# Feed-forward gates written in block order by ScalarE, output weights in two runs, memory tokens copied in that order and begun sooner

## The chip, the cores and the metric

One of the eight cores of a Trainium2 chip runs the kernel. The metric is the device time of one execution in microseconds; of several runs the median is given. One profiled execution gives the rows that are quoted.

## The reference

Two layers of a decoder trunk work on x, 256 tokens of width 1024, in f32. Each layer has a feed-forward step, a mixer of three branches and a second feed-forward step, each with a norm before and after:

```
x += 0.5 * post1(SwiGLU1(pre1(x)))
h  = pre2(x)
x += post2( W_o( sum_i sigmoid(G_i h) * P_i(branch_i(h)) ) )
x += 0.5 * post3(SwiGLU2(pre3(x)))

def swiglu(h, w_in, w_out):
    a, b = split(h @ w_in, 2)            # 2 x 2816 columns
    return (silu(a) * b) @ w_out         # 2816 rows
```

The third branch is cross-attention into 256 memory tokens mem. Its keys and values are rms_norm(mem, mem_g) @ w_mem_kv, with weights and gain of the layer and the same mem in both layers.

## The kernel before

**Tiles and streams.** The 256 tokens are two tiles of 128 (t = 0 and 1). Each is a stream, a Python generator that goes through both layers; the main loop lets the two take turns, stream 0 a few steps ahead, so that a weight tile that was loaded serves both. A step is, for one token tile, one weight tile's products in TensorE. `now` counts the steps. Smaller jobs (the memory tokens' keys and values, attention, compression) are generators in a background list; one piece of them runs after each step, and a number that a generator yields is the count of steps until its next piece. `later(n, fn)` runs fn n steps on.

**Weights.** All products are in f32r with three passes: weight high by x high, weight low by x high, weight high by x low. A weight tile is loaded by SP into one of 4 raw buffers (128 x 1024); `split_unit` then makes whi by a cast on ScalarE (L319) and wlo by a subtraction on VectorE (L320). A dry run of the program finds at what step each tile is first wanted; loads go out up to 7 steps ahead of that and splits up to 4 (AHEAD), in this order and as buffers come free. The instruction orders of the other engines follow from the program's order and the scheduler; each engine works its own list in order.

**Feed-forward** (`ffn`). The columns of w_in go in five pairs of 512 and one of 256. For each, `gate` takes the two accumulators pa and pb: ScalarE makes th = tanh(pa r/2) (L570), VectorE makes (th + 1) pa (L571) and then multiplies by a per-token scale and by pb (L575) into one half of `wide`. Every second gate hands `wide` to `turn_beside`, which brings its 128-column blocks to the transposed form that the second product needs.

**Turning without TensorE.** `turn` has VectorE transpose 32 x 32 squares (L433, tile `blocks`), then one step later (AWAY) four DMAs from GpSimd's queue move the squares' rows to their partitions (L439, tile `moved`), and some steps later (SPLIT = 11) the result is used: for the gates cast and subtracted into turnhi and turnlo (L456, L457). Read with steps (32, 1), column 32q + j of a block of 128 ends on partition 4j + q. So the rows of w_out must lie on the partitions in the same order. Together with the order in which `moving` reads the columns of w_in, this makes w_out's 128 rows come in runs: `RUNS` holds the length u, and the load (L305) reads "(k v u) n -> k u v n", with u = 16 for both feed-forward steps (eight runs of 16 rows for each weight tile) and 64 for w_mix_out and two of the branches.

**Memory tokens** (`memory`). It begins when stream 0 is at the fifth output weight of the first feed-forward step of a layer (`begin_layer`). In layer 0, for each of two tiles (mt), SP loads m; three steps on come its norm (L467 and a chain on GpSimd) and `turn` with order (1, 4), where VectorE reads m with a step of four elements, so that tokens' columns end in plain order; 11 steps later `gained` multiplies by the gain (mf, L710) and makes mThi and mTlo (L713, L714), and `keep` stores the turned tile to DRAM (mthere, L696). Layer 1 reads it back. One step after the last tile the products with w_mem_kv begin, four steps for the keys and four for the values, two steps between, each step with 12 products beside those of the streams.

In layer 0 the steps from the beginning to the products are 3 + 11 + 3 + 11 + 1 = 29, in layer 1 6 + 6 + 1 = 13.

Of the kernel before, what the change touches and what calls it, by code (L numbers as in the profile page):

```python
# [27 lines left out]
AF = mybir.ActivationFunctionType  # L28
OP = mybir.AluOpType
AX = mybir.AxisListType  # L30

P = 128
# [23 lines left out]
LANES = 4  # L56
NORM_B, NORM_C = 1, 1
AWAY, SPLIT, RETURN = 1, 11, 6
CONV, BS, CMP, ZC, QS_0, QS_1, QM, PC, YM = 4, 4, 6, 2, 2, 6, 2, 3, 1
ATT_A, ATT_B, ATT_C, ATT_D, ATT_T = 1, 3, 2, 6, 8  # L60
EARLY, RAMP, SCALES, STAGED, SETUP = 6, 10, 5, 8, 30
PACE, PACE_1, PACED = 9, 8, ("nsa", "memory")

RUNS = {"ffn1_w_out": 16, "ffn2_w_out": 16, "w_mix_out": 64, "w_branch_conv": 64, "w_branch_mem": 64}
PRE = ("ffn1_norm_pre", "mix_norm_pre", "ffn2_norm_pre", "mem_norm")

INV_FREQ = [float.fromhex(v) for v in (
# [39 lines left out]
def view(ap, off, dims):  # L107
    if isinstance(ap, Nothing):
        return ap
    return bass.AP(tensor=ap.tensor, offset=ap.offset + off, ap=[list(ap.ap[0])] + [list(d) for d in dims])  # L110
# [16 lines left out]
def lanes_in(ap, c, n=P):  # L127
    return view(ap, c, [[P, n // P], [1, 4], [4, 32]])


def lanes_out(ap, c, dims):
    return view(ap, c, [list(d) for d in dims] + [[32, 4], [1, 32]])


def f32(ap):
    return ap.bitcast(F32)
# [19 lines left out]
def program(tc, nc, pools, a, out, plan):  # L156
# [18 lines left out]
    def bank(name):  # L175
        return psa.tile([P, 512], F32, name=name, tag="a")
# [4 lines left out]
    def gtile(name, dt=F32):  # L181
        return gp.tile([P, 1024], dt, name=name, tag="g")

    def ttile(name, dt=F32):
        return tp.tile([P, 520], dt, name=name, tag="tmp")
# [55 lines left out]
    order, found, ready = [], {}, {}  # L241
# [30 lines left out]
    def load(item, engines=None):  # L272
# [10 lines left out]
        for off, step, name, l, k0, nk, c0, n in parts:  # L283
# [16 lines left out]
            else:  # L300
                src = a[name][l, k0 * P:(k0 + nk) * P, c0:c0 + n]
                if name in RUNS:
                    rows = src.rearrange("(k v u) n -> k u v n", k=nk, u=RUNS[name])
                    for k in range(nk):
# [61 lines left out]
    def later(delay, fn):  # L366
        serial[0] += 1
        deferred.append((now[0] + delay, serial[0], fn))
# [15 lines left out]
    def product(hT, name, l, cols):  # L384
        ps = [bank("acc") for _ in cols]
        for k in range(8):
            parts = [(0, -1, name, l, k, 1, cols[0][0], cols[0][1])]
            hi, lo = unit((name, l, cols[0][0], k), parts)
            for i, (x2, w) in enumerate(((0, hi), (1, hi), (0, lo))):
                for j, p in enumerate(ps):  # L390
                    n = cols[j][1]
                    pinned(nc.tensor.matmul(p[:, :n], lhsT=hT[x2][:, k], rhs=moving(w, j * n, n),  # L392
                                            start=(k == 0 and i == 0), stop=(k == 7 and i == 2)))
            yield 0
        return ps
# [30 lines left out]

    def turn(src, n, finish, wait, order=(32, 1)):
        f = n // 4  # L430
        make = gtile if n > 512 else ttile
        blocks = make("blocks")
        nc.vector.transpose(blocks[:, :n], view(src, 0, [[order[0], 4], [P, n // P], [order[1], 32]]))  # L433
        moved = []

        def away():
            moved.append(make("moved"))
            for q in range(4):
                nc.gpsimd.dma_start(moved[0][:, q * f:(q + 1) * f],  # L439
                                    blocks[q * 32:(q + 1) * 32, :n].rearrange("j (p f) -> j p f", p=4))  # L440

        later(AWAY, away)
        later(wait, lambda: finish(turned_view(moved[0], n)))
        return moved

    def turned_view(moved, n):
        return view(moved, 0, [[32, n // P], [n // 4, 4], [1, 32]])
# [4 lines left out]
    def turn_beside(src, n, put, wait=SPLIT):  # L452
        def split(mv):
            hi, lo = gtile("turnhi", F32R), gtile("turnlo", F32R)
            hv, lv = quarters(hi[:, :n], n // P), quarters(lo[:, :n], n // P)
            nc.scalar.copy(hv, mv)  # L456
            nc.vector.tensor_sub(lv, mv, f32(hv))  # L457
            put(hi, lo)

        turn(src, n, split, wait)  # L460
# [102 lines left out]
    def ffn(t, l, which):  # L563
        w_in, w_out = f"ffn{which}_w_in", f"ffn{which}_w_out"
        hT, (_, r_half, r2_half, _) = yield from prenorm(x[t], f"ffn{which}_norm_pre", l, t == 0 and l == 0 and which == 1)
        gT, wide = [None] * 3, [None]

        def gate(j, n, pa, pb):
            th = ttile("th")
            nc.scalar.activation(th[:, :n], pa[:, :n], AF.Tanh, scale=r_half)  # L570
            nc.vector.scalar_tensor_tensor(th[:, :n], th[:, :n], 1.0, pa[:, :n], op0=OP.add, op1=OP.mult)  # L571
            if j % 2 == 0:
                wide[0] = gtile("wide")
            both, c0 = wide[0], j % 2 * 512
            nc.vector.scalar_tensor_tensor(both[:, c0:c0 + n], th[:, :n], r2_half, pb[:, :n], op0=OP.mult, op1=OP.mult)  # L575
            if j % 2 == 1:
                turn_beside(both, c0 + n, lambda hi, lo: gT.__setitem__(j // 2, (hi, lo)))

        for j in range(5):
            pa, pb = yield from product(hT, w_in, l, [(j * 512, 512), (DFF + j * 512, 512)])  # L580
            gate(j, 512, pa, pb)
        ps = yield from halves(hT, w_in, l, [(2560, 256), (DFF + 2560, 256)])
        gate(5, 256, ps[:, 0:256], ps[:, 256:512])
        y = [bank("y0"), bank("y1")]
        def between(k):
            if k == 4 and t == 0 and which == 1:
                begin_layer(l)

        def lhs(k):
            c = (k % 8) * P  # L590
            return [v[:, c:c + P] for v in gT[k // 8]]

        yield from output(y, w_out, l, 22, lhs, between)
        yield from postnorm(y, t, (f"ffn{which}_norm_post", l), 0.5, which == 2 and l == DEPTH - 1)
# [97 lines left out]
    def keep(mt, gained):  # L692
        def finish(mv):
            gained(mv)
            whole = bass.AP(tensor=mv.tensor, offset=mv.offset, ap=[list(mv.ap[0]), [1, 1024]]) if not dry else mv
            nc.gpsimd.dma_start(mthere[mt], whole)  # L696
        return finish
# [6 lines left out]
    def memory(l):  # L704
        S = shared[l]
        H = []
        for mt in range(2):
            def gained(mv, scale=[mscale[mt][:, i:i + 1] for i in range(4)]):
                hf, hi, lo = gtile("mf"), gtile("mThi", F32R), gtile("mTlo", F32R)
                nc.vector.tensor_tensor(quarters(hf, 8), mv,  # L710
                                        view(gT, PRE.index("mem_norm") * 16 + l * 8, [[1, 8], [0, 4], [0, 32]]),
                                        op=OP.mult)
                nc.scalar.copy(hi, hf)  # L713
                nc.vector.tensor_sub(lo, hf, f32(hi))  # L714
                H.append((tokens_last(hi, lo), scale))

            if l == 0:
                m = gtile("m")
                nc.sync.dma_start(m, a["mem"][0, mt * P:(mt + 1) * P, :])
                yield 3  # L720
                norm_scales(m, 0, mscale[mt])
                turn(m, 1024, keep(mt, gained), SPLIT, (1, 4))
                yield SPLIT
            else:
                back(mt, gained)
                yield RETURN
        yield 1
        ps = [bank("acc") for _ in range(2)]

        def products(c0):  # L730
            for u in range(4):
                hi, lo = unit(("w_mem_kv", l, c0, u), [(0, 512, "w_mem_kv", l, 2 * u, 2, c0, 512)])
                for mt in range(2):
                    product2(ps[mt], H[mt][0], hi, lo, 512, 2 * u, u == 0, u == 3)
                yield 1

        yield from products(0)
        ks = gtile("ks")
        for mt in range(2):
            nc.scalar.activation(lanes_out(ks, mt * P, [[256, 4]]), lanes_in(ps[mt], 0, 512), AF.Copy,  # L740
                                 scale=H[mt][1][0])

        def keys(hi, lo):
            S["km"] = [v.rearrange("p (h m) -> p h m", h=4) for v in (hi, lo)]

        turn_beside(ks, 1024, keys, KEYS)
        yield 2
        ps = [bank("acc") for _ in range(2)]
        yield from products(512)
        S["vm"] = []  # L750
        for mt in range(2):
            vm = gtile("vm", F32R)
            evac_split(vm[:, 0:512], vm[:, 512:1024], ps[mt], H[mt][1][1])
            S["vm"].append(vm)
# [675 lines left out]
```

## Time and profile before

| | us |
|---|---|
| median of 3 runs | 1219.95 |
| the runs | 1216.92, 1219.95, 1220.46 |
| profiled execution, its time | 1217.41 |
| profiled execution, its span | 1215.7 |
| TensorE busy | 1188.8 |
| VectorE busy | 906.1 |
| ScalarE busy | 722.9 |
| GpSimd busy | 175.4 |

The span goes from the first instruction to the last; the time takes in what lies around it. A TensorE product is pipelined with the next, so its row's duration is longer than its step, and a busy TensorE can still be slowed: the starts of the rows tell. In a row of the timeline stand the start in us from the beginning of the span, the duration, engine, line, operation, tiles (out<-in), shapes and count, and in brackets how long the engine was idle before and what ended that. In a row of a stretch stand its bounds and length, the busy us of PE (TensorE), PEld (its weight loads), DVE (VectorE), ACT (ScalarE) and POOL (GpSimd), the mean granted clock of TensorE, the busy share of the DMA engines and GB/s. In a row of waits stand who waited, for whom, the total, the number of times and the longest. In a row of DMA issues stand the number, the size and the median us from issue to landing.

### The profile page before, as it was taken

To read this page: it belongs to the slowest core of one execution; us is meant where nothing else is said; L and a number is where in the kernel's file an instruction comes from. 1 tells how busy PE (TensorE), PEld (TensorE's weight loads), DVE (VectorE), ACT (ScalarE), POOL (GpSimd) and SP (SyncE) were. 2 spreads that over 40 slices of the span, in tenths; PEclk is the share of its full clock that TensorE was granted. 3 is DMA by queue.
4 is the path that set the end of the run, shared out by engine and by line. 5 is a ranking of instruction groups with operands and counts; after the bars stand their busy time and mean duration, and the time that the engine had idled before them with its cause. 6 is when DMAs were issued, how large, how long until landed. Compare 5 with 4: busy or idle time off the path is not lost. (4 is left out here: it accounts for less than half of the span.)

```text
span 1215.7 us, 16522 instructions
## 1 busy us (share of the span) xinstructions
PE 1188.8 (98%) x5776; PEld 1033.6 (85%) x5776; DVE 906.1 (75%) x1157; ACT 722.9 (59%) x1141; POOL 175.4 (14%) x341
## 2 busy tenths in 40 slices
PE   8999989999999999999999999999999999999996
PEld 7888868988888888888888888888888888888885
DVE  7867667888998776666577677577899976767753
ACT  7555346887986564554464454568878754645541
POOL 4001321321111010011011011013012100110100
PEclk9999999999999999999999999999999999999999
DMA  7878887777478657779957789857757677577992
GB/s 249 271 232 213 207 238 246 218 232 214 145 239 218 217 163 231 233 206 215 270 174 236 221 218 268 228 153 225 239 157 224 194 237 211 185 235 218 211 215 71
DMA packets 127090, 260.63 MB, mean 214 GB/s; under 512 B 11200, under 2 KB 30304, under 8 KB 127008
## 3 DMA queue, kind: packets, MB, share of 16 engines
q1 hardware_dynamic: 117088, 234.58, 66.1%
q0 software_dynamic: 9600, 24.47, 8.1%
q8 instruction: 45, 0.74, 0.3%
q10 hardware_dynamic: 320, 0.53, 0.1%
q14 instruction: 37, 0.30, 0.1%
HBM read 235.42 MB, written 2.10 MB: 195 GB/s over the span
## 5 line engine op out<-in xcount | busy, mean ns | idle before, releaser
L320 DVE TENSOR_TENSOR wlo<-raw,whi 128x1024 fp32r<-128x1024 f32 (+2 forms) x441 | 529.9, 1212 | 172.5 <-ACT whi L319 170.0
L319 ACT CAST whi<-raw 128x1024 fp32r<-128x1024 f32 (+2 forms) x441 | 452.8, 1038 | 275.4 <-PE acc L392 132.8
L439 POOL DMA_DIRECT2D moved<-blocks x176 | 96.3, 565 | 665.5 <-DVE blocks L433 259.7
L392 PE MATMUL acc<-whi,hThi 128*128 128x512 f32 x640 | 191.2, 380 | 0.7 <-ACT whi L319 0.6
L392 PE MATMUL acc<-wlo,hThi 128*128 128x512 f32 x640 | 191.7, 380 | 0.1
L392 PE MATMUL acc<-whi,hTlo 128*128 128x512 f32 x640 | 191.0, 380 | 0.0
L380 PE MATMUL acc<-whi,hThi 128*128 128x512 f32 (+1 forms) x480 | 182.7, 381 | 0.7 <-ACT yf L908 0.4
L381 PE MATMUL acc<-wlo,hThi 128*128 128x512 f32 (+1 forms) x480 | 179.4, 374 | 0.9 <-DVE wlo L320 0.9
L382 PE MATMUL acc<-whi,hTlo 128*128 128x512 f32 (+1 forms) x480 | 179.4, 374 | 0.1
L392 PEld LDWEIGHTS acc<-whi,hThi 128*128 128x128 f32 x640 | 120.4, 189 | 18.6 <-ACT whi L319 0.9
L392 PEld LDWEIGHTS acc<-whi,hTlo 128*128 128x128 f32 x640 | 120.7, 189 | 18.2 <-DVE hTlo L496 1.3
L392 PEld LDWEIGHTS acc<-wlo,hThi 128*128 128x128 f32 x640 | 120.9, 189 | 17.4 <-DVE wlo L320 0.5
L381 PE MATMUL y<-wlo,turnhi 128*128 128x512 f32 x352 | 133.8, 380 | 1.6 <-DVE wlo L320 1.6
L380 PE MATMUL y<-whi,turnhi 128*128 128x512 f32 x352 | 133.6, 380 | 0.0
L382 PE MATMUL y<-whi,turnlo 128*128 128x512 f32 x352 | 133.6, 379 | 0.0
L380 PEld LDWEIGHTS acc<-whi,hThi 128*128 128x128 f32 x480 | 90.7, 189 | 12.1 <-ACT yf L908 0.8
L382 PEld LDWEIGHTS acc<-whi,hTlo 128*128 128x128 f32 x480 | 90.7, 189 | 12.2 <-DVE hTlo L496 0.3
L381 PEld LDWEIGHTS acc<-wlo,hThi 128*128 128x128 f32 x480 | 90.8, 189 | 11.6 <-DVE wlo L320 1.5
L457 DVE TENSOR_TENSOR turnlo<-moved,turnhi 128x1024 fp32r<-128x1024 f32 (+1 forms) x42 | 49.2, 1171 | 58.0 <-ACT turnhi L456 57.9
L456 ACT CAST turnhi<-moved 128x1024 fp32r<-128x1024 f32 (+1 forms) x42 | 42.2, 1006 | 66.1 <-DMA moved<-blocks 64.9
L381 PEld LDWEIGHTS y<-wlo,turnhi 128*128 128x128 f32 x352 | 66.5, 189 | 11.6 <-DVE wlo L320 2.3
L380 PEld LDWEIGHTS y<-whi,turnhi 128*128 128x128 f32 x352 | 66.5, 189 | 9.7 <-ACT whi L319 0.4
(304 smaller groups left out, 1443.2 us busy)
## 6 DMA issues: line engine op xcount, KB each, us to landing
raw<-in_ffn_w_in_dram SPq DMA_DIRECT2D x159, 512.0 KB, 4.8
raw<-in_w_mix_in_dram SPq DMA_DIRECT2D x96, 512.0 KB, 4.6
raw<-in_ffn_w_out_dram SPq DMA_DIRECT2D x88, 512.0 KB, 7.0
moved<-blocks POOLq DMA_DIRECT2D x144, 128.0 KB, 4.4
raw<-in_ffn_w_in_dram SPq DMA_DIRECT2D x33, 256.0 KB, 4.0
raw<-in_w_mem_kv_dram SPq DMA_DIRECT2D x16, 512.0 KB, 5.9
raw<-in_w_mix_out_dram SPq DMA_DIRECT2D x16, 512.0 KB, 4.1
raw<-in_cmp_k_w_dram SPq DMA_DIRECT2D x8, 512.0 KB, 4.5
```

The lines of the kernel that those rows point to most:

```text
L319: pinned(nc.scalar.copy(hi[:, c0:c1], raw[:, c0:c1]))
L320: pinned(nc.vector.tensor_sub(lo[:, c0:c1], raw[:, c0:c1], f32(hi[:, c0:c1])))
L380: nc.tensor.matmul(ps, lhsT=xh, rhs=wh, start=start, stop=False, skip_group_check=skip)
L381: nc.tensor.matmul(ps, lhsT=xh, rhs=wl, start=False, stop=False, skip_group_check=skip)
L382: nc.tensor.matmul(ps, lhsT=xl, rhs=wh, start=False, stop=stop, skip_group_check=skip)
L392: pinned(nc.tensor.matmul(p[:, :n], lhsT=hT[x2][:, k], rhs=moving(w, j * n, n), start=(k == 0 and i == 0), stop=(k == 7 and i == 2)))
L439: nc.gpsimd.dma_start(moved[0][:, q * f:(q + 1) * f], blocks[q * 32:(q + 1) * 32, :n].rearrange("j (p f) -> j p f", p=4))
L456: nc.scalar.copy(hv, mv)
L457: nc.vector.tensor_sub(lv, mv, f32(hv))
```

## The change

Three edits go together.

1. In `gate`, ScalarE writes th in the order of the block moves: it reads pa with a step of four (`lanes_in`) and writes four runs of 32 per block (`lanes_out`). A second ScalarE instruction makes half = pa times the per-token scale in the same order. VectorE then makes (th + 1) half from the two tiles, and multiplies by pb, read with a step of four. The turned columns thereby lie in the order of `moving` alone, and w_out's rows come in two runs of 64 instead of eight of 16.
2. A memory tile is copied by ScalarE into mp in that order, and VectorE transposes mp with the ordinary order; `turn` loses its parameter.
3. In layer 0 the second memory tile is begun 5 steps after the first one's turn instead of 11, and in both layers the products begin 3 steps after the last tile instead of 1: 3 + 5 + 3 + 11 + 3 = 25 steps instead of 29 in layer 0, 6 + 6 + 3 = 15 instead of 13 in layer 1.

```diff
+MSTEP, MWAIT = (5, 11), 3
...
-RUNS = {"ffn1_w_out": 16, "ffn2_w_out": 16, "w_mix_out": 64, "w_branch_conv": 64, "w_branch_mem": 64}
+RUNS = {"ffn1_w_out": 64, "ffn2_w_out": 64, "w_mix_out": 64, "w_branch_conv": 64, "w_branch_mem": 64}
...
-    def turn(src, n, finish, wait, order=(32, 1)):
+    def turn(src, n, finish, wait):
...
-        nc.vector.transpose(blocks[:, :n], view(src, 0, [[order[0], 4], [P, n // P], [order[1], 32]]))
+        nc.vector.transpose(blocks[:, :n], view(src, 0, [[32, 4], [P, n // P], [1, 32]]))
...
         def gate(j, n, pa, pb):
             th = ttile("th")
-            nc.scalar.activation(th[:, :n], pa[:, :n], AF.Tanh, scale=r_half)
-            nc.vector.scalar_tensor_tensor(th[:, :n], th[:, :n], 1.0, pa[:, :n], op0=OP.add, op1=OP.mult)
+            nc.scalar.activation(lanes_out(th, 0, [[P, n // P]]), lanes_in(pa, 0, n), AF.Tanh, scale=r_half)
+            half = ttile("half")
+            nc.scalar.activation(lanes_out(half, 0, [[P, n // P]]), lanes_in(pa, 0, n), AF.Copy, scale=r2_half)
+            nc.vector.scalar_tensor_tensor(th[:, :n], th[:, :n], 1.0, half[:, :n], op0=OP.add, op1=OP.mult)
             if j % 2 == 0:
                 wide[0] = gtile("wide")
             both, c0 = wide[0], j % 2 * 512
-            nc.vector.scalar_tensor_tensor(both[:, c0:c0 + n], th[:, :n], r2_half, pb[:, :n], op0=OP.mult, op1=OP.mult)
+            nc.vector.tensor_tensor(lanes_out(both, c0, [[P, n // P]]), lanes_out(th, 0, [[P, n // P]]),
+                                    lanes_in(pb, 0, n), op=OP.mult)
...
                 norm_scales(m, 0, mscale[mt])
-                turn(m, 1024, keep(mt, gained), SPLIT, (1, 4))
-                yield SPLIT
+                mp = gtile("mp")
+                nc.scalar.copy(lanes_out(mp, 0, [[P, 8]]), lanes_in(m, 0, 1024))
+                turn(mp, 1024, keep(mt, gained), SPLIT)
+                yield MSTEP[mt]
             else:
                 back(mt, gained)
                 yield RETURN
-        yield 1
+        yield MWAIT
```

## The prediction

> **What bounds the kernel now.** I read the page's busy shares first, then TensorE's waits, the timelines of the one region that they pointed to, the busy time by stretches, and last the DMA issues.
>
> ```profile
> span 1215.7 us, 16522 instructions
> PE 1188.8 (98%) x5776; PEld 1033.6 (85%) x5776; DVE 906.1 (75%) x1157; ACT 722.9 (59%) x1141; POOL 175.4 (14%) x341
> ```
> TensorE is busy for 98% of the span, the other engines have a quarter of it or more to spare. Only what lets TensorE wait less or run faster shortens the run. Its waits over the whole run (in total, times, longest) hold two lines that belong to the first layer's memory stage:
>
> ```profile
> PE acc L380 <- ACT whi L319: 3.3, 1, 3.3
> PE y L381 <- DVE wlo L320: 1.6, 2, 0.8
> ```
> The second counts two waits in the output products y of all eight feed-forward passes, and both lie in the stretch below: no other output stage waits. TensorE's timeline there (start us, duration, wait in brackets):
>
> ```profile
> 143.41 0.38 PE L382 MATMUL y<-whi,turnlo 128*128 128x512 f32 x1
> ...
> 145.02 0.48 PE L381 MATMUL y<-wlo,turnhi 128*128 128x512 f32 x1 [0.78 <-DVE wlo L320]
> 145.34 0.38 PE L382 MATMUL y<-whi,turnlo 128*128 128x512 f32 x1
> ...
> 155.27 0.38 PE L380 MATMUL y<-whi,turnhi 128*128 128x512 f32 x1
> 156.45 0.48 PE L381 MATMUL y<-wlo,turnhi 128*128 128x512 f32 x1 [0.80 <-DVE wlo L320]
> 156.77 0.38 PE L382 MATMUL y<-whi,turnlo 128*128 128x512 f32 x1
> ...
> 174.04 0.38 PE L381 MATMUL y<-wlo,turnhi 128*128 128x512 f32 x1
> 174.25 0.38 PE L382 MATMUL y<-whi,turnlo 128*128 128x512 f32 x1
> 177.95 0.79 PE L380 MATMUL acc<-whi,mThi 128*128 128x512 f32 x1 [3.32 <-ACT whi L319]
> 179.40 0.79 PE L381 MATMUL acc<-wlo,mThi 128*128 128x512 f32 x1 [0.66 <-DVE wlo L320]
> 179.99 0.63 PE L382 MATMUL acc<-whi,mTlo 128*128 128x512 f32 x1
> ...
> 183.40 0.57 PE L381 MATMUL acc<-wlo,mThi 128*128 128x512 f32 x1
> 183.81 0.38 PE L382 MATMUL acc<-whi,mTlo 128*128 128x512 f32 x1
> ```
> Undisturbed, one product follows another after 0.215 us (174.04 to 174.25; the rows are rounded). So I count starts, not busy time. From 174.25 to 183.81 there are 12 products (174.25, 177.95, 179.40 and nine from 179.99 to 183.40): 9.56 us where 2.58 would do, a loss of 6.98. From 143.41 to 145.34 three products (one, at 143.76, is not shown) take 1.93 instead of 0.65, a loss of 1.28; from 155.27 to 156.77 two take 1.50 instead of 0.43, a loss of 1.07. Together **9.3 us**, far more than the bracketed waits, because after the long one the clock was down:
>
> ```profile
> 174.30:177.00 2.70, 0.33 (x2) 0.00 (x0) 1.24 (x2) 1.09 (x2) 0.54 (x1) 0.99 0.44 174
> 177.00:184.00 7.00, 5.39 (x12) 3.97 (x13) 5.75 (x5) 3.74 (x4) 0.00 (x0) 0.52 0.53 144
> ```
> By stretches, the granted clock (third number from the right) is 0.99 up to 177.0 and 0.52 in the 7 us behind it: nine steps (179.99 to 183.81) take 3.82 us where 1.94 would do, so 1.9 of the 6.98 is clock. TensorE's last product before it started at 174.25, took 0.38, and the clock fell some 2.4 us later. [...]
>
> **Why it waits.** ScalarE, VectorE and GpSimd in that region:
>
> ```profile
> 136.41 0.83 ACT L456 CAST turnhi<-moved 128x768 fp32r<-128x768 f32 x1 [6.72 <-DMA moved<-blocks]
> 175.91 1.04 ACT L713 CAST mThi<-mf 128x1024 fp32r<-128x1024 f32 x1 [6.62 <-DVE mf L710]
> 176.86 3.88 ACT L319 CAST whi<-raw 128x1024 fp32r<-128x1024 f32 x4
> 158.58 2.91 DVE L433 STREAM_TRANSPOSE blocks<-m 128x1024 f32<-128x1024 f32 x1
> 174.65 1.23 DVE L710 TENSOR_TENSOR mf<-moved,gT 128x1024 f32<-128x1024 f32 x1 [4.10 <-DMA moved<-blocks]
> 166.90 0.56 POOL L439 DMA_DIRECT2D moved<-blocks  x1
> ```
> Engines run in order. ScalarE stops 6.6 us at mThi for mf, which waits for the block moves of the second memory tile (last issued at 166.90, used at 174.65, 7.75 us). Behind mThi stand the weight splits whi that TensorE needs next. At 136.41 it was the same with the block moves of a feed-forward pass's last columns. So slow DMAs are the root, and these rows show why they are slow here:
>
> ```profile
> 391.00:411.00 20.00, 20.00 (x98) 17.46 (x97) 13.75 (x16) 10.23 (x12) 0.00 (x0) 1.00 0.68 215
> 1150.00:1180.00 30.00, 30.00 (x141) 26.27 (x140) 16.82 (x16) 12.65 (x14) 3.34 (x7) 1.00 0.97 216
> raw<-in_ffn_w_out_dram SPq DMA_DIRECT2D x88, 512.0 KB, 7.0
> raw<-in_w_mix_out_dram SPq DMA_DIRECT2D x16, 512.0 KB, 4.1
> moved<-blocks POOLq DMA_DIRECT2D x144, 128.0 KB, 4.4
> moved<-blocks POOLq DMA_DIRECT2D x8, 96.0 KB, 8.1
> ```
> The first stretch loads w_mix_out, whose rows already come in two runs of 64; the second loads ffn w_out in eight runs of 16. At the same 215 GB/s the DMA engines are busy 0.68 of the time in the one and 0.97 in the other, and a 512 KB load lands after 4.1 against 7.0 us. The 128 KB block moves land after 4.4 us in the median of the whole run; the smaller 96 KB ones of this stage (window 120 to 180 us) after 8.1, because they share those engines.
>
> **The change part by part.**
>
> *Row order of w_out.* 88 loads move the same bytes. I take the two-run price: about 0.68/0.97 = 0.70 of the engine time, 4 to 5 us to land. Bounds: 4.1 (as w_mix_out) and 7.0 (no gain, if the price came from what runs beside). On its own it is worth nothing in the seven output stages where TensorE does not wait. In the memory stage it takes up to 8.1 - 4.4 = 3.7 us off a block move, and the first two stalls (0.78 and 0.80 us, both behind such a late move) disappear: 1.28 + 1.07 = 2.35 us.
>
> *Memory copy in lane order.* Per tile (2 of them, first layer only) ScalarE gains one 128x1024 copy, VectorE's transpose loses its stride of four.
>
> ```profile
> L433 DVE STREAM_TRANSPOSE blocks<-wide 128x1024 f32<-128x1024 f32 x16 | 19.8, 1238 | 0.0
> L740 ACT ACTIVATE ks<-acc,mscale 128x512 f32<-128x512 f32 x4 | 2.6, 685 | 1.5 <-PE acc L382 1.5
> L570 ACT ACTIVATE th<-acc,rs 128x512 f32<-128x512 f32 x40 | 27.4, 685 | 14.5 <-PE acc L392 14.4
> L575 DVE SCALAR_TENSOR_TENSOR wide<-th,rs,acc 128x512 f32<-128x512 f32 x40 | 29.9, 748 | 3.3
> ```
> The transpose goes from 2.91 to 1.24, -1.67 us. The copy: ks already reads in lane order and takes 685 ns like the straight th, so I take a straight 1024 cast, 3.88/4 = 0.97 us; the other end is the transpose's own ratio for such a read, 0.97 x 2.91/1.24 = 2.3 us. The chain to the move is 0.7 us shorter, or 0.6 longer at the dear end.
>
> *MSTEP and MWAIT.* The second tile is begun 6 steps sooner (5 instead of 11), and two steps more (3 instead of 1) lie between the last gained tile and the products; a step of y is six products, 1.29 us. The products come 4 steps sooner in all in the first layer, 2 later in the second. Each load, copy, transpose and four moves of the second tile go with it: SP issues its 512 KB six steps earlier, ahead of w_out rows, which then land about 512 KB / 216 GB/s = 2.4 us later once; GpSimd issues the second tile's moves before the first tile's store to DRAM (512 KB) instead of behind it. ScalarE's copy now stands ahead of the first tile's mThi with whi casts behind it. What covers these is the DMA time set free: at 0.70 of the price the 8 to 9 loads in 25 us of such a stage leave about a quarter of the engines, 6 us, against 2.4.
>
> *The long stall.* Last move 7.75 us - 3.3 (at 4.4) and -0.7 for the chain: mf ready 4.0 us sooner. The whi at 176.86 moves to 172.9, and the product that came 1.09 us behind it to 174.0, before TensorE runs dry at 174.25 + 0.215. The margin, 0.5 us, is small, but the two extra steps put 2.6 us of other products in between. At the dear end of the copy a wait of about 0.8 us is left without them, too short for the clock to fall. So I take the whole 6.98.
>
> *The gates.* 48 more ScalarE ops, 40 x 0.685 + 8 x 0.47 (two thirds of it) = 31 us, and VectorE's last step reads PSUM at stride four: 748 ns now (the read scalar goes, some 60 ns less), at worst 748 x 2.91/1.24 = 1.76 us, 45 us more over the run. Both lie beside the products, where ScalarE is idle 41% and VectorE 25% of the span; the accumulators come free about 0.7 us later (1.7 at worst), and no wait of TensorE in the profile is for a free accumulator. Cost zero; if the cover were gone, 0.7 us a gate. [...]
>
> *Sum*, against the profiled execution of 1217.41 us (span 1215.7): -6.98 - 2.35 = -9.3; back on the other side I put 1.5 us, for the second tile's load among w_out rows and for ScalarE, which still stops at both mThi. 1217.4 - 7.8 = 1209.6. The runs shown are 1216.92, 1219.95 and 1220.46, so the profiled one is at the fast end; I add 0.9 for that: **1210.5 us**, 9.5 below the median, 0.8%. 0.3% (3.7 us) is about what a measurement tells from no change.
>
> **The rivals.**
>
> *Nothing to see (1217 to 1220).* The order of the rows is not what costs; the 0.97 would come from the moves beside. Then mf is only 0.7 us sooner, the clock still falls, and 1 to 3 us are saved: 1217. Against it: the same bytes per second at 0.68. For it: the moves are in that stretch alone. 0.18.
>
> *Slower.* The second tile's load is pulled into the stage's fullest stretch, with VectorE's or ScalarE's in-order stop at its junk and copy now ahead of the first tile. If loads stay at 7 us, the stall at 145.02 grows by 2.4 us to 3.2 and costs a clock fall of its own (1.9 us), the one at 156.45 grows by 2.4 as well, and the long stall stays: 1217.4 + 6.7 = 1224. It decides where w_out rows are not cheaper. 0.09.
>
> *More than the stage.* Every instruction behind 140 us is put in a new order, and the mixers, whose waits lie elsewhere, may gain or lose 2 to 3 us: 1206 to 1208 at the good end. 0.10.
>
> **How the numbers follow.** Likeliest case 0.63, 1207 to 1215; with the good end 0.73. Faster by over 0.3% (under 1216.3): 0.73. Within 0.3%: 0.18. Slower: 0.09. The range goes from 1205 (all 9.3 back and some 2 of the mixers) to 1218, the middle of the second case, and leaves out about 0.18.
>
> **What would show it.** Landing of w_out 4 to 5 us instead of 7.0, DMA share in the last output stage near 0.7; transpose of the memory copy at 1.24 us, its copy at 1.0; no granted clock under 1 behind the start; TensorE's wait for whi before the first mThi product gone; the gate's VectorE step below 1 us. The prediction is wrong if w_out still lands in 7 us, if a stall near 145 us grows, or if TensorE begins to wait for gates.

## The result, and the profile after

| | median us | runs | profiled run | span | mean granted clock |
|---|---|---|---|---|---|
| before | 1218.66 (1216.92 to 1220.46) | 4 | 1217.41 | 1215.7 | 0.995 |
| after | 1208.69 (1208.41 to 1209.53) | 4 | 1208.45 | 1206.7 | 0.997 |

The ratio is 0.9919, interval 0.9901 to 0.9938: 10.0 us less by the medians, 9.0 by the two profiled runs. The forecast was 1210.5 in 1205 to 1218.

The busy shares on the page of after, and the DMA issues of w_out over the whole run (last number: median us to landing):

```profile
span 1206.7 us, 16607 instructions
...
PE 1185.5 (98%) x5776; PEld 1031.8 (85%) x5776; DVE 901.2 (75%) x1157; ACT 754.1 (62%) x1191; POOL 171.8 (14%) x341
...
raw<-in_ffn_w_out_dram SPq DMA_DIRECT2D x88, 512.0 KB, 4.5
```

The same 88 loads land in 4.5 us instead of 7.0, and ScalarE has 31 us more to do, as forecast. Two stretches by windows (busy us of PE, PEld, DVE, ACT, POOL, each with its instructions; granted clock; DMA share; GB/s): the first layer's memory stage, before and after, then the last output stage of after.

```profile
140.00:200.00 60.00, 54.45 (x237) 45.72 (x236) 38.54 (x35) 29.58 (x36) 13.28 (x22) 0.94 0.85 239
```
```profile
140.00:200.00 60.00, 60.00 (x280) 52.54 (x279) 39.29 (x38) 34.06 (x40) 7.30 (x15) 1.00 0.80 261
1150.00:1180.00 30.00, 30.00 (x140) 26.27 (x139) 15.53 (x13) 13.01 (x13) 0.00 (x0) 1.00 0.66 210
```

In the same 60 us TensorE now starts 280 products instead of 237: 43 x 0.215 = 9.2 us, practically the whole gain. Its clock is 1.00 where it was 0.94. In the output stage the DMA engines are busy 0.66 for 210 GB/s, where it took 0.97 for 216.

One change gave a little back. TensorE's waits in after, 180 to 220 us, where before had none:

```profile
PE acc L381 <- ACT hThi L496: 0.5, 1, 0.5
PE pt L424 <- DVE x L544: 0.2, 1, 0.2
```

To say where time went I use a sum over TensorE's product starts, worked out from the trace: for each, the distance to the next start beyond the tenth percentile of products of the same line and shape. It holds about 1 us of no wait in 200 to 220; the differences count.

| lost, us | 140 to 200 | 200 to 220 | rest of the run | all |
|---|---|---|---|---|
| before | 9.5 | 1.4 | 47.1 | 58.0 |
| load_order_only | 0.9 | 1.1 | 45.7 | 47.7 |
| memory_only | 5.6 | 3.4 | 46.4 | 55.4 |
| rows_only | 2.1 | 1.0 | 45.8 | 48.9 |
| no_copy | 0.2 | 4.3 | 45.2 | 49.7 |
| after | 0.2 | 3.2 | 45.4 | 48.8 |

Before to after: 9.3 won in the stage, 1.8 given back just behind it, 1.7 won in the rest of the run. That is 9.2 in all, against 9.0 between the profiled times.

### The profile page after: what moved, and what is told of

The parts are those of the page before. It is cut to its first block, busy times and chain, and to the rows that moved or that the text cites. A ratio compares the mean times of both kernels' runs of the same rounds, so it can differ in the third digit from the quotient of the medians.

```text
span 1206.7 us, 16607 instructions
## 1 busy us (share of the span) xinstructions
PE 1185.5 (98%) x5776; PEld 1031.8 (85%) x5776; DVE 901.2 (75%) x1157; ACT 754.1 (62%) x1191; POOL 171.8 (14%) x341
## 2 busy tenths in 40 slices
DMA packets 127091, 260.63 MB, mean 216 GB/s; under 512 B 11200, under 2 KB 30304, under 8 KB 127008
## 4 chain that ended last, share of the span: by engine, by line
PE 81%; DVE 8%; ACT 6%; issue 3%; DMA 1%; POOL 1%; DVEq 0%; SPq 0%; POOLq 0%; ACTq 0%
PE acc L393 34%; PE y L383 7%; PE y L382 7%; PE y L381 7%; PE acc L383 6%; PE acc L381 6%; PE acc L382 6%; DVE wlo L321 2%; ACT whi L320 2%; PE br L381 2%; PE br L382 2%; PE br L383 2%; PE pt L424 1%; PE s L975 1%; DVE QT L857 1%
## 5 line engine op out<-in xcount | busy, mean ns | idle before, releaser
L321 DVE TENSOR_TENSOR wlo<-raw,whi 128x1024 fp32r<-128x1024 f32 (+2 forms) x441 | 529.9, 1210 | 195.5 <-ACT whi L320 193.2
L383 PEld LDWEIGHTS y<-whi,turnlo 128*128 128x128 f32 x352 | 66.5, 189 | 9.4
L457 ACT CAST turnhi<-moved 128x1024 fp32r<-128x1024 f32 (+1 forms) x42 | 42.3, 1006 | 47.2 <-DMA moved<-blocks 46.4
```

Source lines behind the costliest of these rows:

```text
L321: pinned(nc.vector.tensor_sub(lo[:, c0:c1], raw[:, c0:c1], f32(hi[:, c0:c1])))
L383: nc.tensor.matmul(ps, lhsT=xl, rhs=wh, start=False, stop=stop, skip_group_check=skip)
```

## The experiments

My theory was that the order of w_out's rows is the whole cause and that everything else in the change is priced near zero. The rivals were that the memory edits remove the long stall, that the copy decides, and that the gates cost or bring something. All times are against runs of the kernel before on the same chip; its median was 1219.53 beside the first four experiments, 1219.21 beside filled, vector_gates and the two other run lengths, and 1220.02 beside the rest.

**Rows and gates alone**, memory tokens as before:

```diff
-RUNS = {"ffn1_w_out": 16, "ffn2_w_out": 16, "w_mix_out": 64, "w_branch_conv": 64, "w_branch_mem": 64}
+RUNS = {"ffn1_w_out": 64, "ffn2_w_out": 64, "w_mix_out": 64, "w_branch_conv": 64, "w_branch_mem": 64}
```
and the gates of the change.

> The kernel before with the new gates and w_out rows in two runs of 64; memory tokens as before (strided transpose, 11 steps for both tiles, products one step after). Theory A (dear w_out loads are the root of the memory stage's stalls): w_out lands in 4.5 us, block moves in the memory stage in 4 to 5 us, the long stall of 3.32 us falls under 1 us, the clock stays up, 1209 to 1212 us. Rival B (the earlier start and the added steps do it): the long stall and the half clock stay, 1216 to 1218 us.

1208.98 us (1208.25 to 1209.97), ratio 0.991 (0.9885 to 0.9935). So the memory edits aren't needed for the gain. One wait is left in the stage, and the clock stays at 1.00 behind it:

```profile
173.89 0.48 PE L381 MATMUL acc<-wlo,mThi 128*128 128x512 f32 x1 [0.95 <-DVE wlo L320]
```

**The memory edits alone**, with the old rows and gates:

```diff
+MSTEP, MWAIT = (5, 11), 3
...
-                turn(m, 1024, keep(mt, gained), SPLIT, (1, 4))
-                yield SPLIT
+                mp = gtile("mp")
+                nc.scalar.copy(lanes_out(mp, 0, [[P, 8]]), lanes_in(m, 0, 1024))
+                turn(mp, 1024, keep(mt, gained), SPLIT)
+                yield MSTEP[mt]
...
-        yield 1
+        yield MWAIT
```

> The change without its first part: old gates, w_out rows in eight runs of 16; memory tokens copied and begun sooner as in the change. Theory A: w_out still lands in 7 us, block moves in 8, ScalarE still stops some 6 us for them, TensorE loses 4 us or more between 130 and 180 us, 1214 to 1219 us. Rival B: loss under 1.5 us, 1209 to 1211 us.

1218.05 us, ratio 0.9981 (0.9962 to 0.9999). The long stall goes, but another comes 10 us sooner, at an output product, and the clock falls again. Timelines of TensorE, VectorE and GpSimd in this kernel, a window, and the loads of w_out from 120 to 180 us:

```profile
168.44 0.79 PE L382 MATMUL y<-wlo,turnhi 128*128 128x512 f32 x1 [3.24 <-DVE wlo L321]
```
```profile
166.02 1.22 DVE L711 TENSOR_TENSOR mf<-moved,gT 128x1024 f32<-128x1024 f32 x1 [5.22 <-DMA moved<-blocks]
167.16 1.22 DVE L321 TENSOR_TENSOR wlo<-raw,whi 128x1024 fp32r<-128x1024 f32 x1
156.27 2.27 POOL L440 DMA_DIRECT2D moved<-blocks  x4
```
```profile
160.00:180.00 20.00, 16.76 (x72) 14.11 (x71) 11.47 (x10) 8.36 (x9) 0.55 (x1) 0.91 0.91 258
raw<-in_ffn_w_out_dram SPq DMA_DIRECT2D x15, 512.0 KB, 8.6
```

This time VectorE holds TensorE up: it stands 5.22 us at mf, for block moves of the second memory tile that were issued by 158.5 us and used at 166.0, with the wlo of the next y product behind it. Moving the work sooner moved the stall with it.

**The load order alone.** Before with only that line, so that the order of the instructions is the same on every engine (the two traces agree in it). The rows of w_out then meet the wrong columns: the run prices the load order and is no version of the kernel.

```diff
-RUNS = {"ffn1_w_out": 16, "ffn2_w_out": 16, "w_mix_out": 64, "w_branch_conv": 64, "w_branch_mem": 64}
+RUNS = {"ffn1_w_out": 64, "ffn2_w_out": 64, "w_mix_out": 64, "w_branch_conv": 64, "w_branch_mem": 64}
```

> The kernel before with one edit: w_out rows loaded in two runs of 64 though the gates still turn in the old order, so that rows of w_out meet the wrong columns; all engines do the same work as before. It prices the load order without the 48 added ScalarE operations. Theory A: within 1 us of rows_only, DMA share in the last output stage 0.75 instead of 0.97. Rival C (the landing of 7 us comes from the block moves beside it, not from the order): landing stays near 7 us and the time near 1218 us.

1207.82 us (1206.99 to 1208.66), ratio 0.99 (0.9875 to 0.9924): the whole gain, with one number changed in a load's access pattern. The stage and the last output stage:

```profile
140.00:200.00 60.00, 60.00 (x284) 52.55 (x283) 42.19 (x42) 31.38 (x42) 11.45 (x20) 1.00 0.80 261
1150.00:1180.00 30.00, 30.00 (x141) 26.27 (x140) 14.57 (x14) 13.31 (x13) 0.00 (x0) 1.00 0.63 199
```

The gates' new order is what lets the rows come in two runs and still meet their columns. By the medians it costs 1.2 us (1208.98 in rows_only against 1207.82 here, with ranges that overlap); that fits the wait of 0.95 us in rows_only, which this run does not have.

**The change without its copy**, transposes of the memory tiles strided as before:

```diff
-                mp = gtile("mp")
-                nc.scalar.copy(lanes_out(mp, 0, [[P, 8]]), lanes_in(m, 0, 1024))
-                turn(mp, 1024, keep(mt, gained), SPLIT)
+                turn(m, 1024, keep(mt, gained), SPLIT, (1, 4))
```

> The change without the copy: VectorE transposes the memory tokens with a stride of four in 2.9 us, as before; rows, gates and steps as in the change. ScalarE saves two copies of 2.9 us. Theory A: within 1 us of the change, 1208 to 1210 us, for nothing waits there any more. Rival D (the shorter transpose matters): a wait of TensorE of 1 us or more between 130 and 180 us, 1211 us or more.

1209.45 us (1208.48 to 1210.62), ratio 0.9913 (0.9888 to 0.9938). By the medians the copy can't be told (1208.69 with it, the ranges overlap). In the profiled run no wait is left in the stage without it either; the waits for the new x behind the stage are 0.49 and 0.61 us, where the change has 0.24.

**Filling the long stall.** If the fall of the clock is a cost of its own, products without a use that keep TensorE busy in the stall of before should save the 1.9 us:

```diff
+        if l == 0:
+            for _ in range(10):
+                ins = nc.tensor.matmul(ps[0], lhsT=ident_r, rhs=view(ident_r, 0, [[0, 4], [1, P]]), start=True, stop=True)
```

> The kernel before with ten idle products of identity (0.215 us each, 2.2 us) on TensorE just ahead of the first memory product, whose accumulator they use and which overwrites it. They fall into the long stall and take its place; the stall itself stays. If the half clock is a price of its own, 1.9 us of products at half speed plus most of the slow start of the first two, the granted clock stays at 1 and the run is 2 to 3 us shorter, about 1217 us. If the clock's record is only a record, the run is as long as before or up to 1 us longer.

A miss: 1221.33 us, ratio 1.0009 (0.9993 to 1.0026). The fill covered only 2.5 us and left two waits behind it; products then came 0.43 us apart up to 184.5 (timeline, and a window round it). The second layer's memory stage had a fall of its own besides: 0.95 from 740 to 760 us, where before has 1.00.

```profile
175.38 2.46 PE L731 MATMUL acc<-ident_r 128*128 128x512 f32 x10
178.94 0.48 PE L380 MATMUL acc<-whi,mThi 128*128 128x512 f32 x1 [1.09 <-ACT whi L319]
180.38 0.48 PE L381 MATMUL acc<-wlo,mThi 128*128 128x512 f32 x1 [0.96 <-DVE wlo L320]
```
```profile
174.00:186.00 12.00, 9.94 (x37) 7.70 (x36) 6.99 (x6) 5.63 (x6) 0.54 (x1) 0.86 0.63 196
```

**A longer fill**: 18 products, of an activation tile instead of the identity.

```diff
-            for _ in range(10):
-                ins = nc.tensor.matmul(ps[0], lhsT=ident_r, rhs=view(ident_r, 0, [[0, 4], [1, P]]), start=True, stop=True)
+            early = H[0][0][0]
+            for _ in range(18):
+                ins = nc.tensor.matmul(ps[0], lhsT=early[:, 0], rhs=early[:, 0:4].rearrange("p k t -> p (k t)"),
+                                       start=True, stop=True)
```

> As filled, but with 18 products (3.9 us) of the first memory tile's own values instead of ten of identity, so that the long stall is filled to its end and TensorE works on real numbers. The first memory product is late by 0.4 us at most. If the clock falls for idle time, it stays at 1 here, the products after the stall step by 0.215 us and the time is 2 us shorter than before's fast runs, about 1217 us, with less scatter. If it falls in spite of the filling, the time is that of before or up to 1 us more.

1220.00 us, ratio 0.9996 (0.9983 to 1.001): the total missed again, but the stage did what was expected.

```profile
180.69 0.38 PE L382 MATMUL acc<-whi,mTlo 128*128 128x512 f32 x1
...
182.63 0.38 PE L382 MATMUL acc<-whi,mTlo 128*128 128x512 f32 x1
```
```profile
174.00:186.00 12.00, 11.14 (x51) 9.20 (x50) 6.99 (x6) 5.67 (x6) 0.54 (x1) 1.00 0.61 188
...
740.00:760.00 20.00, 18.22 (x76) 15.11 (x75) 13.03 (x12) 9.38 (x10) 0.00 (x0) 0.91 0.89 239
```

The clock stayed at 1.00. The nine steps that the prediction counted at half clock (3.82 us) take 1.94 us here, so 1.9 us of the stall was clock, as the prediction had it. From the last y product to the twelfth memory product it is 7.86 us instead of 9.56; the first memory product comes 0.66 us later behind the fill. The total did not move: in the profiled run the second layer's memory stage got waits of 1.22 and 0.56 us and a fall of its own (0.91 there, 1.00 before). Every engine works in the same order as in before; what came later is the memory tile read back from DRAM, which landed in 10.4 us instead of 9.1. Whether other runs of before have this fall too isn't known, since only one execution is profiled.

**Gates with other arithmetic**, rows in two runs, memory as before. VectorE does both products, each with a read of PSUM at a step of four, and ScalarE only the tanh:

```diff
-            half = ttile("half")
-            nc.scalar.activation(lanes_out(half, 0, [[P, n // P]]), lanes_in(pa, 0, n), AF.Copy, scale=r2_half)
-            nc.vector.scalar_tensor_tensor(th[:, :n], th[:, :n], 1.0, half[:, :n], op0=OP.add, op1=OP.mult)
+            nc.vector.tensor_scalar(th[:, :n], th[:, :n], 1.0, r2_half, op0=OP.add, op1=OP.mult)
+            nc.vector.tensor_tensor(tv, tv, lanes_in(pa, 0, n), op=OP.mult)
```

> w_out rows in two runs of 64, memory tokens as before, gates without the second ScalarE operation: ScalarE writes th in block order, VectorE makes (th + 1) times the scale, then multiplies by pa and by pb, both read from PSUM with a step of four (three VectorE operations instead of two, one ScalarE instead of two). It takes 31 us from ScalarE and gives VectorE about 25 us. Theory A: nothing waits for the gates, so the time is that of rows_only within 1 us, 1208 to 1210 us. If ScalarE's added work delayed the splits in rows_only (its one stall of 0.95 us between 160 and 180 us), 1207 to 1208 us. If VectorE is the shorter blanket, 1211 us or more.

1208.30 us (1207.04 to 1209.44), ratio 0.99 (0.9881 to 0.9919), not to be told from the change. Against rows_only, ScalarE is busy 25 us less and VectorE 17 us more, and neither shows: both engines are covered.

**What the two schedule numbers do by themselves**, on top of rows and gates. First only the wait, then only the step:

```diff
+MSTEP, MWAIT = (11, 11), 3
```
```diff
+MSTEP, MWAIT = (5, 11), 1
```

> rows_only with MWAIT = 3 alone (both tiles' steps 11, products 2 steps later than before). If the memory products cover the change of stream 0 from feed-forward to mixer at 195 to 215 us (theory E), TensorE has no wait there, the 0.95 us wait of rows_only between 160 and 180 us is gone too, 1207 to 1208.5 us. If the waits at 200 to 220 us of the change come from its other edits, they show up here as well: 1209 us or more.

> rows_only with MSTEP = (5, 11) alone (second tile begun 6 steps sooner, products one step after the last tile, so 6 steps earlier than before). Theory E: the memory products end before stream 0 changes to the mixer, TensorE waits there 1 us or more in the profile and loses 2 us or more in starts between 200 and 220 us, 1209 to 1211 us. Otherwise 1207 to 1208.5 us.

1208.84 us (1207.77 to 1211.13), ratio 0.9913 (0.9898 to 0.9928), and 1209.92 us (1209.07 to 1210.27), ratio 0.9916 (0.9902 to 0.9931). The first expectation missed its place, the second held. Each removes the 0.95 us wait at 173.9 (rows_wait leaves 0.14) and opens another. TensorE's waits of the two, 140 to 220 us:

```profile
PE pt L424 <- DVE x L544: 1.4, 1, 1.4
```
```profile
PE acc L381 <- ACT hThi L496: 1.2, 1, 1.2
PE pt L424 <- DVE x L544: 0.3, 1, 0.3
```

Counted in TensorE's order: in rows_only two batches of 12 memory products (2.6 us each) stand, among others, between each stream's last output product and the transposes pt of its new x, and in both streams nothing waits. In rows_wait stream 0 has one batch and six output products there, and waits 1.44 us; in rows_step no memory products are left by then. So the memory products seem to have been cover for the change from feed-forward to mixer. The count alone does not settle it, though: the change has the same one batch and six products for stream 0 and does not wait there. In rows_wait ScalarE starts the squares of stream 0's output (junk), of which its new x is made, 2.2 us or more behind the start of the last output product, in the change the later one 0.4 us behind. For stream 1 the change has no memory products left, and it waits 0.24 and 0.53 us.

**Both together, other gates and `MWAIT = 3`**, as a candidate for a better kernel, vector_gates with

```diff
+MSTEP, MWAIT = (11, 11), 3
```

> vector_gates with MWAIT = 3 alone: no second ScalarE operation, no copy, products 2 steps later. By theory E nothing is lost against vector_gates and little is left to win: 1207 to 1208.5 us, at or just under the change.

1212.34 us (1209.86 to 1212.75), ratio 0.9933 (0.9919 to 0.9947): a miss, slower by the median than vector_gates and than rows_wait (whose range it overlaps). The wait for x grew to 1.94 us at 193.2 and the clock fell behind it:

```profile
180.00:200.00 20.00, 18.06 (x80) 15.10 (x79) 15.74 (x18) 12.16 (x21) 2.79 (x5) 0.91 0.83 268
```

No version run here beats the change clearly.

**Other run lengths**, one run each and with rows that meet the wrong columns, before with 32 rows a run (four runs), then with 8 (sixteen):

```diff
+RUNS = {"ffn1_w_out": 32, "ffn2_w_out": 32, "w_mix_out": 64, "w_branch_conv": 64, "w_branch_mem": 64}
```
```diff
+RUNS = {"ffn1_w_out": 8, "ffn2_w_out": 8, "w_mix_out": 64, "w_branch_conv": 64, "w_branch_mem": 64}
```

> The kernel before with w_out rows loaded in four runs of 32 (rows meet the wrong columns; all engines do the same work). If the price rises with the number of runs, landing between 4.5 and 7 us and DMA share in the last output stage between 0.75 and 0.97. If eight runs are special, as with two runs: 4.5 us, 0.75.

> The kernel before with w_out rows loaded in sixteen runs of 8 (rows meet the wrong columns; all engines do the same work). If the price rises with the number of runs, landing above 7 us, TensorE waits in every output stage and the run is longer than before. If it is set by something that eight runs already have in full, near 7 us and 0.97.

1210.19 us and 1288.85 us. Four runs cost about what two do: w_out lands in 4.5 us and an output stage has a DMA share of 0.76 at 222 GB/s, where load_order_only has 0.75 at 226 in the same window. Sixteen runs are far worse, in another way. First the window of four runs, then one of sixteen, and SP's queue over the whole of before and of load_runs_8 (packets, MB, share):

```profile
1140.00:1170.00 30.00, 30.00 (x141) 26.27 (x140) 18.94 (x19) 14.04 (x15) 4.34 (x8) 1.00 0.76 222
```
```profile
120.00:140.00 20.00, 20.00 (x94) 17.48 (x93) 10.44 (x13) 6.57 (x8) 2.17 (x4) 1.00 0.63 162
```
```profile
q1 hardware_dynamic: 117088, 234.58, 66.1%
```
```profile
q1 hardware_dynamic: 116384, 234.58, 60.2%
```

With sixteen runs ScalarE waits 165 us in all for loads of w_out, and yet the 16 DMA engines are only 0.63 busy at 162 GB/s; in the same window of before, with eight, the share is 1.02 at 247 (it counts packets' time over 16 engines' and can pass 1). So the price is not so much per run. SP's queue has 704 packets fewer with the same bytes, which is eight for each of the 88 loads, and the packets under 512 bytes are 704 fewer too (10496 in all queues against 11200). No row here shows single engines, so why they stand idle with sixteen runs was not shown.

## Why the prediction was right, point by point

**Row order (right; all of the gain).** 4 to 5 us to land were forecast, 4.5 came; 0.70 of the engine time was forecast, 0.66/0.97 = 0.68 came (0.70 at equal bytes). load_order_only shows that this term is the cause. The rival by which the order of rows costs nothing falls with it, and so does the slower one, which asked for loads that stay at 7 us: memory_only shows what those do (8.6 us in the stage and a 3.24 us stall).

**The first two stalls and the long one (right).** No wait of TensorE is left between 100 and 200 us. 9.3 us were forecast for all three; the starts give 9.3. The margin of the long one was not put to the test as the prediction put it (a wait of about 0.8 us without the two extra steps and with a dear copy): rows_only, with none of the memory edits, keeps a wait of 0.95 us, and rows_step, with the earlier start but neither the extra steps nor the copy, keeps none. In before the waits of 0.78 and 0.80 us left the clock at 1.00 from 140 to 160 us.

**The block moves (right in sum by luck, by other parts).** The 96 KB moves at 8.1 us, from which the prediction read the stage's price, are those of the feed-forward's last 768 columns; a memory tile's are the 128 KB ones, 5.9 us in the same window of before. The second stall stood behind mThi of the first memory tile, so behind moves of that size too. The forecast had mf 4.0 us sooner, 3.3 of it in the moves. DMA issues of after, 120 to 180 us, and the steps of the second memory tile on ScalarE, VectorE and GpSimd:

```profile
moved<-blocks POOLq DMA_DIRECT2D x8, 128.0 KB, 4.6
moved<-blocks POOLq DMA_DIRECT2D x8, 96.0 KB, 3.9
```
```profile
143.04 2.92 ACT L727 COPY mp<-m 128x1024 f32<-128x1024 f32 x1
145.99 1.25 DVE L434 STREAM_TRANSPOSE blocks<-mp 128x1024 f32<-128x1024 f32 x1 [2.58 <-ACT mp L727]
147.54 2.27 POOL L440 DMA_DIRECT2D moved<-blocks  x4 [0.38 <-DVE blocks L434]
154.39 1.23 DVE L714 TENSOR_TENSOR mf<-moved,gT 128x1024 f32<-128x1024 f32 x1 [0.37 <-DMA moved<-blocks]
```

From the copy's start to mf it is 11.35 us; from the transpose of before (158.58) to its mf (174.65) it was 16.07, so 4.7 less. Copy and transpose cost 1.3 us more (4.2 instead of 2.9). The four moves, which before stood between small operations of GpSimd from 162.06 on, come back to back: from the transpose's end to the last move's end it is 2.6 us instead of 6.0, which the prediction had not counted. The landing gives the last 2.6.

**The copy (wrong).** "I take a straight 1024 cast, 3.88/4 = 0.97 us; the other end is ... 2.3": it takes 2.90 us, outside both ends.

```profile
L727 ACT COPY mp<-m 128x1024 f32<-128x1024 f32 x2 | 5.8, 2904 | 0.0
L434 DVE STREAM_TRANSPOSE blocks<-mp 128x1024 f32<-128x1024 f32 x2 | 2.5, 1246 | 5.1 <-ACT mp L727 5.1
```

The row that I put nearest, ks, reads the accumulators in PSUM at that step; the copy reads SBUF. The chain of copy and transpose became 1.3 us longer instead of 0.7 shorter. Why the copy took 2.90 us where a straight cast from SBUF took 0.97 was not shown. It cost no time that shows: no product in the stage waits for it, and no_copy, without it, has no wait there either.

**The gates at zero (right).** Groups of after:

```profile
L574 DVE SCALAR_TENSOR_TENSOR th<-th,half 128x512 f32<-128x512 f32 x40 | 27.7, 692 | 14.1 <-ACT half L573 14.1
L578 DVE TENSOR_TENSOR wide<-th,acc 128x512 f32<-128x512 f32 x40 | 27.5, 687 | 2.8
L571 ACT ACTIVATE th<-acc,rs 128x512 f32<-128x512 f32 x40 | 27.4, 685 | 13.8 <-PE acc L393 13.5
L573 ACT ACTIVATE half<-acc,rs 128x512 f32<-128x512 f32 x40 | 27.2, 679 | 0.0
```

VectorE's read of PSUM at a step of four takes 687 ns, where the straight one with a scalar more took 748 and the straight one of pa (L571 of before) 683. The worst case of the prediction, 1.76 us by the transpose's ratio for a read of SBUF, came on neither engine. The zero is close rather than exact: rows_only is 1.2 us above load_order_only.

**The 1.5 us "back on the other side" (right in size by luck, wrong in place).** It was put down to the second tile's load and to mThi. What came is 1.8 us at 200 to 220, at the new x and hThi, where memory products no longer stand for stream 1. The 1.7 us won in the rest of the run stand in no term of the sum, only in the third rival; they are spread over many small differences, and their cause is open.

**The baseline.** I added 0.9 us to get from the profiled run to a median; the after runs agree within 1.1 us, and its profiled run is one of them. Without that step the forecast is 1209.6.

## What to carry to other kernels

When loads of the same size land at different speeds, compare the DMA busy share at equal GB/s and take the price from the sibling with another row order: here that alone carried the whole gain, and it is worth a run by itself before any schedule is touched. Schedule edits made around a symptom move the stall while the cause stands, and are worth nothing once it is gone; and work that is moved may stop covering what it covered, so count in the engine's own order what will stand in the old place. Price a strided read from a row with the same memory, not merely the same step: at a step of four ScalarE took 685 ns for 512 columns from PSUM, like the straight read, but 2.90 us for 1024 from SBUF against 0.97.

## What the runs showed of the hardware that was not expected

- A 512 KB load of 128 rows in eight runs of 16 lands in 7.0 us with the DMA engines 0.97 busy; in four runs of 32 or two of 64 it lands in 4.5 with 0.63 to 0.76. What makes eight runs dear is open.
- From SBUF, ScalarE's copy with a read at a step of four fp32 took 3.0 times a straight cast of the same size (2.90 against 0.97 us) and VectorE's transpose 2.3 times the straight one (2.91 against 1.24); from PSUM neither engine showed a price (ScalarE 685 ns either way, VectorE 687 against 683).
- Two waits of 1.09 and 0.96 us behind the fill were followed by 3.4 us at half clock (0.50 from 182 to 184 us), while two of 0.99 and 0.97 us in load_runs_32 were followed by none. In the traces of before and after the granted clock's records, all but the last of each, are whole multiples of 3.413 us long: in before 170.67, 6.83 and 1027.41 us (50, 2 and 301 times), in after 1194.67 (350 times). In stretches of 3.41 us counted from where a record ends, both waits of filled lie in one, with TensorE busy 1.35 us, and those of load_runs_32 in two (first row, then the other two). The falls of before and memory_only follow stretches with 1.09 and 0.49 us busy. That it counts where a wait falls is my inference from these few stretches. A sharp limit isn't shown: filled has a fall behind a stretch with 1.79 us busy, load_runs_8 none behind one with 1.42.

```profile
177.76:181.17 3.41, 1.35 (x6) 0.89 (x6) 3.20 (x3) 3.41 (x5) 0.00 (x0) 1.00 0.21 85
```
```profile
170.66:174.07 3.41, 2.42 (x11) 1.67 (x9) 2.30 (x3) 2.39 (x3) 0.54 (x1) 1.00 0.38 154
174.07:177.48 3.41, 2.44 (x12) 2.04 (x12) 3.41 (x4) 2.45 (x3) 0.00 (x0) 1.00 0.28 46
```

- The seventeen runs of before beside the first experiments spread over 11 us, with mean granted clocks from 0.992 to 0.997; those of rows_only lie within 1.8 us at 0.997 to 0.998. Much of the scatter of before would then be falls of the clock, which is inferred from these means alone.
